# Delta rule with one inversion: ordering the loads of the inverted blocks and the first products on them

## The chip, the cores and the metric

The kernel runs on one core of a Trainium2 chip. The metric is the device time of one execution in microseconds (us); the median of three runs of the kernel before is 1357.24 us. TensorE is called PE here, VectorE DVE, ScalarE ACT, GpSimd POOL and SyncE SP.

## What is computed

The program runs two blocks on 256 tokens of width 1024 (the first block on 272, with 16 meta tokens): a feed-forward layer, an mLSTM mixer and a feed-forward layer, and then a gated delta rule mixer, a convolution-gated feed-forward layer, sliding-window attention and another such feed-forward layer. Only the delta rule is touched. Its core in the reference, for each chunk of 64 tokens and each of 16 heads:

```python
m = jnp.where(strict, jnp.einsum('bnhcd,bnhsd->bnhcs', k_beta, k) * decay, 0.0)
t_mat = lax.linalg.triangular_solve(m + eye, eye, left_side=True, lower=True, unit_diagonal=True)
u = jnp.einsum('bnhcs,bnhse->bnhce', t_mat, v_beta)
w = jnp.einsum('bnhcs,bnhsd->bnhcd', t_mat, k_beta * jnp.exp(gc)[..., None])
```

A step over the chunks then uses `u` and `w`; a gated norm and an output projection follow.

## The kernel before, in words

**Weights.** All weights lie in one tensor, in halves of eight 128x128 tiles (512 KB). `load_half` (L159) starts the transfer of a half into one of four `raw` buffers (L164) and keeps the transfer in `lastw[0]`. ACT then casts the half to `whi` in two pieces (L172), and DVE or POOL subtracts to get `wlo` (L174), into one of five pairs of buffers. `wtile` (L195) asks for the half that is `LOOK` = 3 ahead of the one in use. In the delta-rule stage the transfers are issued by ACT (L1150 sets `wq[0]` to it), elsewhere by SP. `mm3` (L248) makes three products for each tile (L251 to L253) and keeps the last one in `lastmm[0]`.

**The delta-rule stage.** Four blocks of projections are made first; 44 more (each eight tiles, so one half, and 24 products) are fillers: the rest of k and q, then z, then v, 16 blocks of each of the last two. I call the v blocks V0 to V15. The output projection `op_all` (L1130) is the last filler: 16 halves, O0 to O15, each of which needs the result of one head. Three halves of the feed-forward layer behind it, N0 to N2, are asked for before the stage ends.

Beside them run chains. `front` (L960) makes the masked products and stores them to DRAM (`ud`). `invert` (L979) loads the 32x32 diagonal blocks (`B`) and inverts all 128 of them at once on POOL, in 31 steps of two operations (L986, L988); the inverses go to DRAM (`xyd`, two POOL transfers, L992), and two more buffers are cleared (L997). `levels(q8)` (L1006), for each of eight head pairs, starts two loads of its off-diagonal rows (L1009) and four loads of inverted blocks (L1012), both on SP's queue, and then doubles the blocks from 32 to 128 by products with X and Y (L1026, L1034, L1048, L1053), of which L1026 is the first. `solve` and `outp` follow (L1067 to L1124). There are three XY buffers, `XYB` and two halves of `XZ`, so levels 0 to 2 begin together when the inversion is marked done, and each later level waits for the level three before it.

A v block ends on ACT (L737), three DVE operations (L739), ACT (L757), DVE (L758), two transposes on PE (L808) and two ACT copies into `Vn` (L810).

**What sets the order.** `Weave` (L48) is a planner in Python: each filler step and each chain step has a cost, a latency and a due time, and the planner puts out a chain's step when its due time has come and filler steps in between. The inversion counts 54 + 9 us there (L39, L999). Until it is marked done, DVE splits all weights; with the same mark POOL takes the odd halves (`share`, L1002). The program so put out is then scheduled at compile time: within the limits of the data and of ordering edges, the scheduler may move an instruction ahead of others on its engine's queue. `after(first, then)` (L144) draws such an ordering edge (class NoSync), which by itself gives no wait on the chip.

Of the kernel before, what the change touches and what calls it, by code (L numbers as in the profile page):

```python
# [120 lines left out]
def stack_kernel(ctx, tc, w, xt, cols, rows, gw, baw, rel, kc, kb, out):  # L121
    nc = tc.nc
    V, S, P_, T_ = nc.vector, nc.scalar, nc.gpsimd, nc.tensor
# [11 lines left out]
    def ps_mm(tag=None):  # L135
        if tag is None:
            rot[0] += 1
            tag = "st" if rot[0] % 3 == 0 else "mm"
        return pp.tile([128, 512], F32, name=tag, tag=tag, bufs=2 if tag == "st" else 4)
# [4 lines left out]
    def after(first, then):  # L144
        tc.add_manual_dep(then.ins, first.ins.name,
                          mybir.DependencyInfo(mybir.DependencyClass.NoSync, mybir.DependencyReason.DATA),
                          reason="order")

    lastw, lastmm = [None], [None]
# [567 lines left out]
    with tc.tile_pool(name="gd", bufs=1) as gp, tc.tile_pool(name="gw", bufs=2) as gq:  # L717
        def unit():
            return gp.tile([128, SEQ], F32, name="u1k", tag="u1k", bufs=67)
# [184 lines left out]
        def urows(g):  # L904
            return bass.AP(tensor=ud.tensor, offset=ud.offset + g * UG, ap=[[128, 128], [UG, 2], [1, 128]])
# [100 lines left out]
        def levels(q8):  # L1006
            u = [unit(), unit()]
            for j in range(2):
                nc.sync.dma_start(out=u[j], in_=urows(4 * q8 + 2 * j))  # L1009
            XY = xyt[q8 % 3]  # L1010
            for a in range(4):
                nc.sync.dma_start(out=XY[32 * a:32 * a + 32, :, 64 * a:64 * a + 64], in_=bass.AP(  # L1012
                    tensor=xyd.tensor, offset=xyd.offset + (16 * q8 + a) * 2048,
                    ap=[[64, 32], [4 * 2048, 4], [1, 64]]))
            fill.sp = max(fill.sp, fill.now) + 2.8
            xyv = XY.rearrange("p g (c t) -> p g c t", t=2)
            X, Y = xyv[:, :, :, 0], xyv[:, :, :, 1]
            yield 0.0, fill.sp + 2.0 - fill.now, 0.0
            def us(g, r0, nr, c0, ncl):
                return u[g // 2][r0:r0 + nr, (g % 2) * 128 + c0:(g % 2) * 128 + c0 + ncl]  # L1020

            r32 = unit()[:, 0:128].rearrange("p (g n) -> p g n", g=4)
            pr = ps_mm("mm")
            for b in (0, 64):
                for g in range(4):
                    T_.matmul(pr[b + 32:b + 64, g * 32:g * 32 + 32], us(g, b, 32, b + 32, 32), X[b:b + 32, g, b:b + 32],  # L1026
                              start=True, stop=True)
            for b in (32, 96):
                S.copy(r32[b:b + 32], pr[b:b + 32, 0:128].rearrange("p (g n) -> p g n", g=4))
            yield 0.5, 0.9, 0.0  # L1030
            px = ps_mm("mm")
            for b in (0, 64):
                for g in range(4):
                    T_.matmul(px[b:b + 32, g * 32:g * 32 + 32], r32[b + 32:b + 64, g, :],  # L1034
                              Y[b + 32:b + 64, g, b + 32:b + 64], start=True, stop=True)
                for g in range(4 if b == 0 else 0):
                    T_.matmul(px[b + 32:b + 64, g * 32:g * 32 + 32], Y[b + 32:b + 64, g, b + 32:b + 64],
                              r32[b + 32:b + 64, g, :], start=True, stop=True)
            for b in (0, 64):
                V.tensor_copy(Y[b:b + 32, :, b + 32:b + 64], px[b:b + 32, 0:128].rearrange("p (g n) -> p g n", g=4))  # L1040
                if b == 0:
                    V.tensor_copy(X[32:64, :, 0:32], px[32:64, 0:128].rearrange("p (g n) -> p g n", g=4))
            yield 1.0, 0.4, 0.9

            r64 = unit().rearrange("p (g n) -> p g n", g=4)
            pr = ps_mm("mm")
            for g in range(4):
                T_.matmul(pr[64:128, g * 64:g * 64 + 64], us(g, 0, 64, 64, 64), X[0:64, g, 0:64], start=True, stop=True)  # L1048
            S.copy(r64[64:128], pr[64:128, 0:256].rearrange("p (g n) -> p g n", g=4))
            yield 0.43, 0.7, 0.0  # L1050
            px = ps_mm("mm")
            for g in range(4):
                T_.matmul(px[0:64, g * 64:g * 64 + 64], r64[64:128, g, :], Y[64:128, g, 64:128], start=True, stop=True)  # L1053
            V.tensor_copy(Y[0:64, :, 64:128], px[0:64, 0:256].rearrange("p (g n) -> p g n", g=4))
            yield 0.43, 0.4, 0.42
            yield from solve(q8, Y)

        def solve(q8, Y):
            n21 = N21.pop(q8)
            pcs = [unit(), unit()]  # L1060
            pc = [pcs[g // 2][:, (g % 2) * 128:(g % 2) * 128 + 128] for g in range(4)]
            fill.need(("v", 2 * q8))
            fill.need(("v", 2 * q8 + 1))
            pw = ps_mm("mm")
            for j in range(2):
                vh = 2 * q8 + j
                T_.matmul(pw[:, j * 128:j * 128 + 128], Y[:, 2 * j], Vn[:, 0, vh, :], start=True, stop=True)  # L1067
                S.activation(out=pc[2 * j], in_=pw[:, j * 128:j * 128 + 128], func=AF.Copy,
                             scale=cc[:, 0, vh:vh + 1])
            yield 0.43, 1.0, 0.0  # L1070
            pw2 = ps_mm("mm")
            for j in range(2):
                T_.matmul(pw2[:, j * 128:j * 128 + 128], n21[:, j * 128:j * 128 + 128], pc[2 * j],
                          start=True, stop=True)
            V.tensor_tensor(out=Vn[:, 1, 2 * q8:2 * q8 + 2, :], in0=Vn[:, 1, 2 * q8:2 * q8 + 2, :],
                            in1=pw2[:, 0:256].rearrange("p (a b) -> p a b", a=2), op=ALU.subtract)
            yield 0.43, 0.4, 0.42
            pw3 = ps_mm("mm")
            for j in range(2):
                vh = 2 * q8 + j  # L1080
                T_.matmul(pw3[:, j * 128:j * 128 + 128], Y[:, 2 * j + 1], Vn[:, 1, vh, :], start=True, stop=True)
                S.activation(out=pc[2 * j + 1], in_=pw3[:, j * 128:j * 128 + 128], func=AF.Copy,
                             scale=cc[:, 1, vh:vh + 1])
            fill.mark("y", q8)
            yield 0.43, 1.0, 0.0
            yield from outp(q8, pc)
# [69 lines left out]
        for q8 in range(8):  # L1156
            cond = [("i",)]
            if q8 >= 3:
                cond.append(("y", q8 - 3))
            fill.chains.append((cond, levels(q8)))  # L1160
# [277 lines left out]
```

## Time and profile before

| | |
|---|---|
| median of 3 runs | 1357.24 us (1354.59 to 1360.41) |
| profiled execution | 1363.15 us, span 1361.4 us |
| PE, PE weight load | 95%, 93% of the span busy |
| DVE, ACT, POOL | 67%, 57%, 9% |
| mean granted TensorE clock | 0.971 of full |
| delta-rule stage | about 560 to 880 us of the span |

The span is what the profiler saw between the first and the last instruction. Busy shares are averages over the whole span; what the change touches lies in one stage, so the stage's own stretches, waits and queues are what is to be read.

### The profile page before, as it was taken

What the parts mean: (1) busy time and instruction counts of PE and PEld (TensorE: products, weight loads), DVE (VectorE), ACT (ScalarE), POOL (GpSimd) and SP (SyncE); (2) the same over time, 40 slices, a digit from 0 to 9 for tenths busy, and PEclk for the clock granted to TensorE, in tenths of its full rate; (3) what the DMA queues carried; (4) which work ended last, traced back from release to release, by engine and by line L of the source; (5) the groups of instructions that cost most, each with busy time, mean ns of one, the idle gap of its engine ahead of it and who ended that gap; (6) DMA issues with size and microseconds to landing.
All of it is one profiled execution on the core that took longest, in us unless ns stands there. A gap on an engine that the chain in (4) does not pass through costs nothing.

```text
span 1361.4 us, 27159 instructions
## 1 busy us (share of the span) xinstructions
PE 1298.9 (95%) x10665; PEld 1259.9 (93%) x10665; DVE 914.1 (67%) x1727; ACT 780.0 (57%) x1805; POOL 129.0 (9%) x149
## 2 busy tenths in 40 slices
PE   9999999999999999999973899999999999999997
PEld 8999999988999999899973789999999988999997
DVE  7866547775777753686662744698896575998852
ACT  7555446654765543556642645676675576777640
POOL 0000000000000000034493102201100000000000
PEclk9999999999999999999996879999999999999998
DMA  7755543532465554224733442468877431466650
GB/s 256 243 173 176 178 155 128 157 122 78 161 212 187 187 186 138 66 94 133 209 101 108 130 124 82 127 172 221 223 215 234 158 107 63 156 222 199 187 167 32
DMA packets 76064, 213.36 MB, mean 157 GB/s; under 512 B 16613, under 2 KB 25349, under 8 KB 75808
## 3 DMA queue, kind: packets, MB, share of 16 engines
q1 hardware_dynamic: 65248, 175.78, 40.9%
q10 hardware_dynamic: 8928, 31.99, 7.4%
q0 software_dynamic: 1760, 3.86, 1.6%
q8 instruction: 84, 1.38, 0.4%
q14 instruction: 44, 0.36, 0.1%
HBM read 207.00 MB, written 4.59 MB: 155 GB/s over the span
## 4 chain that ended last, share of the span: by engine, by line
PE 84%; DMA 4%; POOL 4%; DVE 3%; ACT 3%; issue 2%; SPq 0%; ACTq 0%; DVEq 0%; POOLq 0%
PE mm L251 13%; PE mm L253 12%; PE mm L252 12%; PE st L251 7%; PE st L252 7%; PE st L253 7%; DMA raw<-in_w 3%; PE mm L269 2%; PE mm L271 2%; PE mm L273 2%; POOL Z L988 2%; POOL tmp L986 2%; PE st L269 1%; PE st L273 1%; PE st L271 1%
## 5 line engine op out<-in xcount | busy, mean ns | idle before, releaser
L172 ACT CAST whi<-raw 128x512 fp32r<-128x512 f32 x752 | 435.8, 616 | 319.6 <-PE mm L252 107.0
L174 DVE TENSOR_TENSOR wlo<-raw,whi 128x1024 fp32r<-128x1024 f32 (+1 forms) x358 | 438.0, 1225 | 156.2 <-ACT whi L172 145.2
L251 PE MATMUL mm<-xh,whi 128*128 128x256 f32 (+1 forms) x1072 | 305.4, 285 | 1.3 <-ACT xh L380 1.3
L253 PE MATMUL mm<-xh,wlo 128*128 128x256 f32 (+1 forms) x1072 | 304.6, 284 | 0.0
L252 PE MATMUL mm<-xl,whi 128*128 128x256 f32 (+1 forms) x1072 | 304.2, 284 | 0.1
L251 PEld LDWEIGHTS mm<-xh,whi 128*128 128x128 f32 x1072 | 202.8, 189 | 3.1 <-ACT xh L380 2.2
L251 PE MATMUL st<-xh,whi 128*128 128x256 f32 (+1 forms) x704 | 202.1, 287 | 1.5 <-DVE gy L739 1.3
L252 PEld LDWEIGHTS mm<-xl,whi 128*128 128x128 f32 x1072 | 202.5, 189 | 0.5 <-DVE xl L381 0.5
L253 PEld LDWEIGHTS mm<-xh,wlo 128*128 128x128 f32 x1072 | 202.7, 189 | 0.1
L253 PE MATMUL st<-xh,wlo 128*128 128x256 f32 (+1 forms) x704 | 201.3, 286 | 0.0
L252 PE MATMUL st<-xl,whi 128*128 128x256 f32 (+1 forms) x704 | 201.0, 286 | 0.0
L251 PEld LDWEIGHTS st<-xh,whi 128*128 128x128 f32 x704 | 134.6, 191 | 2.6 <-DVE gy L739 1.5
L253 PEld LDWEIGHTS st<-xh,wlo 128*128 128x128 f32 x704 | 134.4, 191 | 0.1
L252 PEld LDWEIGHTS st<-xl,whi 128*128 128x128 f32 x704 | 134.5, 191 | 0.0
L251 PE MATMUL mm<-hh,whi 128*128 128x256 f32 (+1 forms) x352 | 99.5, 283 | 0.0
L252 PE MATMUL mm<-hl,whi 128*128 128x256 f32 (+1 forms) x352 | 99.4, 282 | 0.0
L253 PE MATMUL mm<-hh,wlo 128*128 128x256 f32 (+1 forms) x352 | 99.4, 282 | 0.0
L174 POOL TENSOR_TENSOR wlo<-raw,whi 128x1024 fp32r<-128x1024 f32 x19 | 45.3, 2384 | 500.4 <-ACT whi L172 434.2
L251 PEld LDWEIGHTS mm<-hh,whi 128*128 128x128 f32 x352 | 67.0, 190 | 0.0
L252 PEld LDWEIGHTS mm<-hl,whi 128*128 128x128 f32 x352 | 66.5, 189 | 0.0
L253 PEld LDWEIGHTS mm<-hh,wlo 128*128 128x128 f32 x352 | 66.5, 189 | 0.0
L440 DVE SCALAR_TENSOR_TENSOR fu<-mm,colt,fu 128x255 f32<-128x255 f32 x108 | 51.3, 478 | 14.5 <-ACT fu L437 14.4
(504 smaller groups left out, 2672.8 us busy)
## 6 DMA issues: line engine op xcount, KB each, us to landing
raw<-in_w SPq DMA_DIRECT2D x317, 512.0 KB, 4.4
raw<-in_w ACTq DMA_DIRECT2D x60, 512.0 KB, 3.8
ud<-u1k SPq DMA_DIRECT2D x16, 128.0 KB, 3.4
u1k<-ud SPq DMA_DIRECT2D x16, 128.0 KB, 3.2
Tb<-bvd POOLq DMA_DIRECT2D x16, 128.0 KB, 5.9
gx<-in_w SPq DMA_DIRECT2D x2, 512.0 KB, 6.7
xyd<-Z POOLq DMA_DIRECT2D x2, 512.0 KB, 5.3
h<-in_xt SPq DMA_DIRECT2D x3, 272.0 KB, 6.1
```

The lines of the kernel that those rows point to most:

```text
L172: S.copy(hi[:, c[0]:c[1]], raw[:, c[0]:c[1]])
L174: (P_ if share[0] and u % 2 else V).tensor_tensor(out=lo[:, c[0]:c[1]], in0=raw[:, c[0]:c[1]], in1=hi[:, c[0]:c[1]].bitcast(F32), op=ALU.s ...
L251: T_.matmul(ps, hi, xhh, start=first, stop=False)
L252: T_.matmul(ps, hi, xll, start=False, stop=False)
L253: lastmm[0] = T_.matmul(ps, lo, xhh, start=False, stop=last)
L269: T_.matmul(pss[j], wts[j][0], xhh, start=(k == 0), stop=False)
L271: T_.matmul(pss[j], wts[j][1], xhh, start=False, stop=False)
L273: T_.matmul(pss[j], wts[j][0], xll, start=False, stop=(k == kt - 1))
L440: V.scalar_tensor_tensor(out=t[:, d:], in0=ps[:, :T - d], scalar=wc(2 - d), in1=t[:, d:], op0=ALU.mult, op1=ALU.add)
L986: P_.tensor_tensor(out=t, in0=X[:, i, 0:i + 1].unsqueeze(1).to_broadcast([128, n, i + 1]), in1=B[:, i, i + 1:32].unsqueeze(2).to_broadcast ...
L988: P_.tensor_tensor(out=X[:, i + 1:32, 0:i + 1], in0=X[:, i + 1:32, 0:i + 1], in1=t, op=ALU.add)
```

## The change

Two ordering edges are added in `levels`. Each of the four loads of inverted blocks of a level is ordered behind the weight load put out last at that point, and the first of the eight L1026 products of each level (b = 0, g = 0) is ordered behind the last product of `mm3` put out by then. No instruction, size or buffer changes.

```diff
             for a in range(4):
-                nc.sync.dma_start(out=XY[32 * a:32 * a + 32, :, 64 * a:64 * a + 64], in_=bass.AP(
+                ins = nc.sync.dma_start(out=XY[32 * a:32 * a + 32, :, 64 * a:64 * a + 64], in_=bass.AP(
                     tensor=xyd.tensor, offset=xyd.offset + (16 * q8 + a) * 2048,
                     ap=[[64, 32], [4 * 2048, 4], [1, 64]]))
+                after(lastw[0], ins)
...
             for b in (0, 64):
                 for g in range(4):
-                    T_.matmul(pr[b + 32:b + 64, g * 32:g * 32 + 32], us(g, b, 32, b + 32, 32), X[b:b + 32, g, b:b + 32],
-                              start=True, stop=True)
+                    ins = T_.matmul(pr[b + 32:b + 64, g * 32:g * 32 + 32], us(g, b, 32, b + 32, 32), X[b:b + 32, g, b:b + 32],
+                                    start=True, stop=True)
+                    if b == 0 and g == 0:
+                        after(lastmm[0], ins)
```

## Rows read from the trace of the kernel before

**Rows 1.** Page, 40 slices of 34 us: busy tenths of PE in each.
```profile
PE   9999999999999999999973899999999999999997
```
**Rows 2.** PE's waits, whole span: line, what it waited for, us, times, longest.
```profile
PE ax L808 <- DVE gy L758: 32.8, 2, 29.6
```
**Rows 3.** Waits of DVE and of ACT, 660 to 900 us.
```profile
DVE gy L758 <- ACT vs L757: 31.6, 4, 30.1
ACT Vn L810 <- DMA XZ<-xyd: 31.9, 1, 31.9
ACT u1k L391 <- DVE gyo L1121: 15.8, 12, 3.3
```
**Rows 4.** Timeline of ACT and its queue at the stall: start, us, what [idle before].
```profile
702.09 0.47 ACT L737 ACTIVATE gy<-st,colt 128x256 f32<-128x256 f32 x1
734.08 0.34 ACTq L164 DMA_DIRECT2D raw<-in_w  x1
734.46 0.37 ACT L810 ACTIVATE Vn<-ax,nkh 128x128 f32<-128x128 f32 x1 [31.90 <-DMA XZ<-xyd]
734.63 0.38 ACTq L164 DMA_DIRECT2D raw<-in_w  x1
```
**Rows 5.** Timeline of SP's queue and of POOL at the end of the inversion.
```profile
728.24 2.91 SPq L1012 DMA_DIRECT2D XYB<-xyd  x4
731.00 1.83 POOL L997 MEMSET XZ<- 128x1024 f32 x2 [5.88 <-DMA xyd<-Z]
731.97 3.63 SPq L1012 DMA_DIRECT2D XZ<-xyd  x8
```
**Rows 6.** The chain that ended last, 724 to 735 us: start, us, what.
```profile
732.32 1.74 DMA XZ<-xyd
```
**Rows 7.** Stretches: length, then busy us of PE, PEld, DVE, ACT, POOL, clock, DMA.
```profile
682.60:702.50 19.90, 19.90 (x170) 19.74 (x169) 18.89 (x28) 13.40 (x32) 18.41 (x20) 1.00 0.46 148
705.90:735.90 30.00, 0.36 (x4) 0.15 (x2) 0.48 (x2) 1.29 (x4) 18.71 (x33) 0.54 0.22 49
735.90:764.90 29.00, 27.28 (x222) 26.33 (x223) 22.71 (x39) 18.40 (x46) 0.00 (x0) 0.95 0.53 168
764.90:798.00 33.10, 26.22 (x297) 23.21 (x296) 16.61 (x42) 21.44 (x75) 4.70 (x2) 0.73 0.48 143
798.00:876.60 78.60, 78.09 (x739) 73.85 (x737) 39.28 (x74) 39.56 (x127) 16.70 (x7) 0.94 0.31 97
```
**Rows 8.** PE's groups, 735 to 766 us: products of the v blocks, one of three.
```profile
L251 PE MATMUL st<-xh,whi 128*128 128x256 f32 x48 | 14.5, 301 | 1.3 <-DVE gy L739 1.3
L251 PE MATMUL ax<-xh,whi 128*128 128x256 f32 x16 | 4.5, 280 | 0.0
```
**Rows 9.** Line 737, 684 to 703 us: durations min/median/max in ns, first and last start.
```profile
L737 ACT ACTIVATE gy<-st,colt x4: 471/473/475, 685.2 to 702.1; 128x256 f32<-128x256 f32 x4
L737 ACT ACTIVATE gy<-ax,colt x2: 457/465/473, 688.3 to 697.0; 128x256 f32<-128x256 f32 x2
```
**Rows 10.** Lines 164 and 174, 733 to 878 us: weight loads on ACT, splits on POOL.
```profile
L164 ACTq DMA_DIRECT2D raw<-in_w x26: 334/334/381, 734.1 to 866.7; - x26
L174 POOL TENSOR_TENSOR wlo<-raw,whi x9: 2337/2382/2406, 767.1 to 871.7; 128x1024 fp32r<-128x1024 f32 x9
```
**Rows 11.** Timeline of ACT, 750 to 765 us: weight loads and v blocks' ends.
```profile
754.93 0.82 ACTq L164 DMA_DIRECT2D raw<-in_w  x2
...
760.77 0.33 ACTq L164 DMA_DIRECT2D raw<-in_w  x1
...
762.45 0.47 ACT L737 ACTIVATE gy<-ax,colt 128x256 f32<-128x256 f32 x1
```
**Rows 12.** Timeline of PE: first products of level 0, and the products behind them.
```profile
740.76 0.59 PE L1026 MATMUL mm<-XYB,u1k 32*32 32x32 f32 x16
...
765.23 0.34 PE L1034 MATMUL mm<-XYB,u1k 32*32 32x32 f32 x5
```
**Rows 13.** Page, DMA issues: KB each, median us from issue to landing.
```profile
raw<-in_w ACTq DMA_DIRECT2D x60, 512.0 KB, 3.8
```

## The prediction

> **What bounds the kernel now.** I read the slices first: PE is full nearly everywhere, and the one hole of the whole program is in slices 21 to 23 [rows 1]; its granted clock is 0.54 there [rows 7]. So the kernel is bound by PE's work, and time can be had only where PE stands. PE's waits name the hole: the transposes of a v block (L808) waited 29.6 us for DVE, in one piece, of 32.8 us of such waits in the program [rows 2]. That releaser is only the last link. DVE in turn waited 30.1 us for ACT's tanh, and ACT waited 31.9 us ahead of a copy into Vn, which needs nothing from DRAM, for a load of inverted blocks, XZ<-xyd [rows 3]. ACT's own timeline shows why: the instruction that stands ahead of that copy is a weight load, issued at 734.08 [rows 4]. The first XZ load leaves SP at 731.97 and lands at 732.32 + 1.74 = 734.06 [rows 5, 6]. The next weight load leaves at 734.63, half a microsecond later [rows 4]. I read that so: ACT's weight load carries a wait on a load of SP's, which stands some places earlier in the scheduled order of transfers. Twelve loads of blocks (levels 0 to 2) left SP's queue together, four XYB and eight XZ [rows 5]; the first XZ is the fifth of twelve, and the weight load would be the thirteenth, eight places on. The second weight load fits the sixth. The blocks themselves cannot come sooner: POOL writes the inverses out, clears XZ from 731.00 on, and only then do the XZ loads go [rows 5]. So ACT, DVE and PE stood for the end of the inversion, though the eight v blocks that were left need nothing of it. In the hole PE worked 0.36 of 30 us and DMA was busy 0.22 of the time [rows 7].
>
> The rule that speaks against this reading is the Trainium skill's, Trainium Kernel Development and Optimization, section Key Constraints: transfers issued by SP, ACT and POOL run on the same 16 DMA engines and interleave. By it, two queues meet in bandwidth, and moving an order between them would give no time at all; with DMA at 0.22 in the hole the trace does not agree that bandwidth was what ACT lacked. What it would give, 1357 us, is the second rival below.
>
> **The change part by part.** It removes and adds no instruction; 32 edges on loads and 8 on first products move things.
>
> *The edges on loads, levels 0 to 2.* Which load is "put out last" there? The same mark that lets the levels start gives POOL the odd halves. After the hole 26 weight loads are left on ACT and POOL makes nine splits, the first at 767.1 [rows 10]. 26 are V9 to V15, O0 to O15 and N0 to N2; of the last 19 nine have odd numbers in the tensor (O1 is the first, V15 is odd too and was split by DVE). So the mark falls after V15's load was put out, which is when V12 starts, and before O1's, when V14 starts; counting the planner's costs through gives the middle of V13, so the edge is to O0's load. All loads that the v blocks need then stand ahead of the twelve loads of blocks, and the wait moves from V9's load to O1's, or further.
>
> What that gives: PE has eight v blocks left after the hole (64 products of one kind in 735 to 766 [rows 8]). Ahead of the hole six blocks ended on ACT in 702.1 - 685.2 = 16.9 us, five steps of 3.4 us [rows 9], with DVE at 18.89 of 19.90 us and PE full [rows 7]. At that pace the last eight take PE from 705.9 to 705.9 + 8 x 3.4 = 733, against 764.9 now. The last block's product end moves by up to 32 us.
>
> What is late next: first O1's load. In the trace it left ACT at 760.77, just ahead of V13's end on ACT at 762.45 [rows 11]. V13 would end on ACT at 702.1 + 8 x 3.4 = 729, so ACT comes to O1's load near 727 and stands until the XZ load lands at 734.1: some 7 us for ACT, and 5 for PE (in the trace 31.9 on ACT made 29.6 on PE). From there on everything runs as it did from 760.77: a shift of 760.77 - 734.08 = **26.7 us**. If O0's load is what waits (the second of the pair at 754.93, so about 755.3 [rows 11]), the shift is 21. If the wait falls behind O1's, the blocks' landing bounds it: the XZ loads leave SP until 735.6 [rows 5] and land 1.7 us later, 737.3, where now the second products of level 0 (L1034) start at 765.23 [rows 12], so 28, and with level 0 going ahead alone (its four loads leave by 731.2 [rows 5]) up to 31. I take 27, the nearest to the rows, and 21 to 31 as its ends.
>
> *The edges on loads, levels 3 to 7.* They are put out when O2's or O3's load was, by the same count; these loads need no buffer that the levels hold, and are long gone when the XY buffers of levels 0 to 2 come free. Cost 0; covered by that buffer wait. If the cover is gone, a load of blocks waits for one weight load, 3.8 us each [rows 13].
>
> *The edges on first products.* Level 0's went ahead of V9's last product at 740.76, yet its result was used at 765.23 [rows 12], after all v blocks. Behind V14's products it still is in time: 0, with 24 us of cover. Levels 1 and 2 are behind V14 and V15 already. For levels 3 to 7 the last product put out is V15's or one of O0's or O1's. The trace has no such wait; bounds: 0, and one block of the output projection, 24 products at 19.9 us / 170 = 0.12 us [rows 7], 3 us for each of five, which only counts where PE stands for it. PE works 78.09 of 78.6 us from 798 on [rows 7], so I take 0, and keep -5 for the range.
>
> *The clock.* The mean of 0.95 in 735.9 to 764.9 [rows 7] means some 2.9 us at half clock (1.2 GHz), so 1.4 us of work lost after the hole. A shorter stand may still halve it: between 0 and +1.4, I take 0. The levels' stretch, at 0.73, and the next, at 0.94 [rows 7], I leave as they are; either could move by 3 us in either direction.
>
> *SP and POOL.* SP's queue keeps its order: loads of rows, twelve loads of blocks, loads of rows for level 3. POOL does the same work. The sum is -27.
>
> **Base.** The profiled execution took 1363.15 us with a span of 1361.4 us; the median of the runs shown is 1357.24, 0.4% lower. I take the shift, which is one wait long, over to the median: 1357.2 - 27 = **1330**. The profiled execution would come to 1336.
>
> **The rivals.**
>
> *A longer stand stays* (gain 8 to 20, about 1343). The scheduler could put O0's or O1's load earlier on ACT than now. It can't before V13's half is split, since there are four raw buffers, and that is at 720 by the same pace; then ACT stands 14 us and PE 12, and the gain is 18; with DVE's backlog behind it less. For it: ACT issues V9's load well ahead of its use. Against: rows 11 have these loads late.
>
> *The edges do not decide* (1357). An edge from ACT's queue to SP's is no wait, and if the scheduled order of the transfers does not change, nothing does. For it: the other uses of `after` in the kernel pair instructions of one engine. Against: the wait in rows 3 and 4 is itself made of such an order.
>
> *More is given back* (gain 33 to 38, about 1322). PE stood 6.9 of 33.1 us in the levels' stretch [rows 7]; if the last v blocks fall into it, some of that is filled.
>
> *Slower* (about 1368). One mechanism: the first products of levels 3 to 7 stand on PE's queue behind products of the output projection, and those wait for the heads' last splits; then each level pays its predecessor's end in series. Such an end showed 3.3 us at the longest (ACT's L391 waiting for DVE's L1121 [rows 3]). It decides against the gain only where five levels lose over 27/5 = 5.4 us each, and by 0.5% at 6.8 us; 8 us each would give 1330 + 40 = 1370. Against: PE is full from 798 on [rows 7], with such products between those of the levels.
>
> **How the numbers follow.** Forecast 0.62; longer stand 0.17; more given back 0.08; edges do not decide 0.08; slower 0.05. The forecast's own range is 1326 to 1337 (31 and 21 less, with clock). The range of 1321 to 1347 takes in the longer stand and most of "more", and leaves out the last two cases and an edge, some 0.16. About 0.5%, 6.8 us, is what a measurement of this kernel can tell from no change; faster than 1350.5 has 0.88, within 0.07, slower than 1364 0.05.
>
> **What would show it.** In the changed kernel: V9's load on ACT's queue before 705 and no wait of over 15 us of ACT for XZ or XYB; PE's wait at L808 down from 29.6 to under 12 us; all v products done by 743; the twelve block loads still at 728 to 736, since POOL's part is the same; the first L1034 at 735 to 744; the stage's end, and all behind it, earlier by the shift. I am wrong if ACT's wait is as long in front of another load, if SP's block loads leave later than 736, or if PE's stands return in front of L1026 or in the output projection.

## The result, and the profile after

The change takes the median from 1357.40 to 1341.87 us (four runs of each): a ratio of 0.9888, with an interval of 0.9856 to 0.9921. It is faster by more than 0.5%, and by 15.5 us where 27 were forecast. The program was measured twice more, once under another edit that compiles to the same order (1341.61 against 1360.20) and once as it is (1342.52 against 1364.40), so its gain lies between 15.5 and 21.9 us, and the forecast was too large by 5 to 12. The profiled execution took 1343.67 us, span 1341.9, mean granted clock 0.979 (before: 1363.15, 1361.4, 0.971). The times of the stage below come from one profile of each program; where the change has three profiles, the text gives all three.

The page's slices after, PE, answering to [rows 1]. The hole of three slices is now a dent of three.

```profile
PE   9999999999999999999998889999999999999997
```

Waits of PE and of ACT after, 660 to 900 us (line, what it waited for, us in total, times, longest), answering to [rows 2, 3]:

```profile
PE mm L1027 <- DMA XYB<-xyd: 4.9, 3, 3.5
PE st L251 <- DVE gy L739: 3.2, 2, 3.0
PE ax L808 <- ACT Vn L810: 2.9, 1, 2.9
PE ax L808 <- DVE gy L758: 0.9, 2, 0.5
...
ACT vs L757 <- DVE gy L739: 16.4, 11, 3.4
ACT Vn L810 <- PE ax L808: 10.1, 4, 8.0
```

The 31.9 us of ACT for XZ and the 29.6 us of PE at L808 are gone. (The change adds lines, so L1026 is L1027 after, and L1034 is L1037.) But a wait that was not there stands first: PE in front of the first product on the inverted blocks.

The timeline after of ACT's weight loads and of two v blocks' ends on ACT (V5 and V13, as in [rows 9, 11]), of POOL and of SP's queue (start, us, what, idle before), answering to [rows 4, 5, 11]:

```profile
702.59 0.33 ACTq L164 DMA_DIRECT2D raw<-in_w  x1
...
704.13 0.47 ACT L737 ACTIVATE gy<-st,colt 128x256 f32<-128x256 f32 x1
...
733.50 0.34 ACTq L164 DMA_DIRECT2D raw<-in_w  x1
...
735.21 0.47 ACT L737 ACTIVATE gy<-ax,colt 128x256 f32<-128x256 f32 x1
...
743.77 0.34 ACTq L164 DMA_DIRECT2D raw<-in_w  x1
...
736.81 1.83 POOL L997 MEMSET XZ<- 128x1024 f32 x2 [6.08 <-DMA xyd<-Z]
...
733.90 3.13 SPq L1012 DMA_DIRECT2D XYB<-xyd  x4
737.78 4.14 SPq L1012 DMA_DIRECT2D XZ<-xyd  x8
```

V9's load leaves at 702.59, where it stood until 734.08 [rows 4]. O1's load leaves at 733.50, 27.3 us earlier than at 760.77 [rows 11]: the forecast's 26.7. But the block loads leave SP 5.7 us *later* than 728.24 and 731.97 [rows 5], and they are longer on the way. The chain that ended last, after (start, us, what), has the first of them:

```profile
733.90 5.04 DMA XYB<-xyd
```

It lands at 738.94. O1's weight load, issued at 733.50, was on the way then, and lands at 738.77. Before, no weight load was on the way, and the same block load took 2.8 us, from 728.24 to 731.05. So the first block is there 7.9 us later than before: 5.7 from leaving later and 2.2 from the longer way.

The timeline after of PE around the first products of level 0, answering to [rows 12], and then the first instruction of the norm that ends the stage, before (first line) and after:

```profile
731.88 0.38 PE L251 MATMUL st<-xh,whi 128*128 128x256 f32 x1 [3.03 <-DVE gy L739]
739.08 0.60 PE L1027 MATMUL mm<-XYB,u1k 32*32 32x32 f32 x8 [3.46 <-DMA XYB<-xyd]
740.97 0.63 PE L1027 MATMUL mm<-XYB,u1k 32*32 32x32 f32 x8
745.62 0.34 PE L1037 MATMUL mm<-XYB,u1k 32*32 32x32 f32 x5
```
```profile
884.77 0.61 PE L344 MATMUL ax<-ones,acc 128*128 128x1 f32 x4
865.38 0.60 PE L344 MATMUL ax<-ones,acc 128*128 128x1 f32 x4
```

So the shift shrinks as one goes down the chain: 27.3 us at O1's load, 765.23 - 745.62 = 19.6 at level 0's second products, 19.4 at the stage's end, 1361.4 - 1341.9 = 19.5 in the span. All that is missing was lost before 746 us. Nothing is lost or won behind that.

The stretches after, as in [rows 7]:

```profile
705.90:735.90 30.00, 25.89 (x199) 24.21 (x197) 27.08 (x41) 18.00 (x44) 22.50 (x31) 0.96 0.55 160
735.90:764.90 29.00, 21.15 (x226) 19.16 (x227) 12.81 (x29) 13.49 (x37) 6.53 (x4) 0.63 0.38 109
764.90:798.00 33.10, 29.24 (x291) 26.95 (x290) 14.76 (x34) 15.55 (x58) 2.40 (x1) 0.80 0.39 119
```

PE works 25.89 us of the old hole (it was 0.36), and the low mean clock that the hole had (0.54) is now in the stretch behind it (0.63), where the recursion of the levels begins.

**Why the blocks come later.** POOL's groups of the inversion, first before, then after (busy us, mean ns of one), 660 to 760 us:

```profile
L988 POOL TENSOR_TENSOR Z<-Z,tmp 128x31 f32<-128x31 f32 (+15 forms) x31 | 22.2, 717 | 2.4
L986 POOL TENSOR_TENSOR tmp<-Z,B 128x31 f32<-128x31 f32 (+15 forms) x31 | 20.9, 674 | 13.2 <-DMA B<-ud 10.8
```
```profile
L988 POOL TENSOR_TENSOR Z<-Z,tmp 128x31 f32<-128x31 f32 (+15 forms) x31 | 26.8, 865 | 2.4
L986 POOL TENSOR_TENSOR tmp<-Z,B 128x31 f32<-128x31 f32 (+15 forms) x31 | 21.0, 679 | 13.6 <-DMA B<-ud 11.2
```

The same 62 operations ran from 673.04 to 720.94 before and from 673.81 to 726.46 after: 52.7 us in place of 47.9. Operation by operation the reason can be read. The same two operations of POOL, before (first two lines) and after, and what DVE did after:

```profile
709.73 0.68 POOL L988 TENSOR_TENSOR Z<-Z,tmp 128x231 f32<-128x231 f32 x1
711.12 0.66 POOL L988 TENSOR_TENSOR Z<-Z,tmp 128x220 f32<-128x220 f32 x1
```
```profile
710.48 1.56 POOL L988 TENSOR_TENSOR Z<-Z,tmp 128x231 f32<-128x231 f32 x1
712.83 1.53 POOL L988 TENSOR_TENSOR Z<-Z,tmp 128x220 f32<-128x220 f32 x1
...
709.85 1.63 DVE L174 TENSOR_TENSOR wlo<-raw,whi 128x1024 fp32r<-128x1024 f32 x1
712.44 1.39 DVE L174 TENSOR_TENSOR wlo<-raw,whi 128x1024 fp32r<-128x1024 f32 x1
```

Each POOL operation of over 1.1 us lies beside a split of DVE: 15 of 62 after, 10 of 62 before. Before, DVE stood idle from 705 on with everything else, so the last part of the inversion ran free. The stall had been speeding up the very work that it waited for.

### The profile page after: what moved, and what is told of

Its sections match the earlier page's. It is cut to its first block, busy times and chain, and to the rows that moved or that the text cites. A ratio compares the mean times of both kernels' runs of the same rounds, so it can differ in the third digit from the quotient of the medians.

```text
span 1341.9 us, 27160 instructions
## 1 busy us (share of the span) xinstructions
PE 1301.2 (97%) x10665; PEld 1260.8 (94%) x10665; DVE 919.1 (68%) x1727; ACT 780.2 (58%) x1805; POOL 134.0 (10%) x149
## 4 chain that ended last, share of the span: by engine, by line
PE 79%; DMA 6%; DVE 5%; ACT 4%; POOL 4%; issue 2%; SPq 0%; ACTq 0%; DVEq 0%; POOLq 0%
PE mm L251 11%; PE mm L253 11%; PE mm L252 11%; PE st L251 7%; PE st L252 7%; PE st L253 7%; DMA raw<-in_w 4%; PE mm L269 2%; PE mm L271 2%; PE mm L273 2%; POOL Z L988 2%; POOL tmp L986 2%; DVE wlo L174 2%; ACT whi L172 1%; PE st L269 1%
```

## The experiments

The theory that I took to the chip: (a) the time before was lost because ACT's weight load waited for a load of blocks of SP's, and the edges on loads alone remove that; (b) of the forecast's gain, part went because DVE's splits now lie beside the inversion, and part because PE meets the first product of level 0 before the blocks are there, with products of V14 and V15 queued behind it. The rivals: the edges on products do part of the work, the transfers only compete for bandwidth, POOL is slowed by something other than DVE, the stand of PE costs nothing.

**The edges on loads alone, and the edges on products alone.**

```diff
-                    if b == 0 and g == 0:
-                        after(lastmm[0], ins)
```

> Only the edges on the loads of inverted blocks; the first products carry no edge. Theory (the load edges do all of it): same as the full change, 1338 to 1346 us, ratio 0.986 to 0.991, first products of level 0 in the middle of V14, PE standing some 3.5 us in front of them. Rival (the product edges bring a part): at least 4 us slower than the full change, with first products of level 0 ahead of V14.

Measured: 1341.61, ratio 0.9861 (0.9836 to 0.9886). In the compiled order this program is the same as the change's, instruction for instruction, so its run is a second one of the change.

```diff
-                after(lastw[0], ins)
```

> Only the edges on the first products; the loads stay where they were in the order. Theory: ACT still waits over 28 us in front of a weight load for a load of blocks, PE still stands 29 us at L808, ratio 0.997 to 1.003. Rival (the order of products on PE is what counted): like the full change, ratio 0.986 to 0.991.

Measured: 1361.17, ratio 1.0001 (0.9983 to 1.0018). ACT's wait is there as before, if a little under the 28 us expected (PE's at L808 is 25.2):

```profile
ACT Vn L810 <- DMA XZ<-xyd: 26.6, 1, 26.6
```

The whole gain is that of the load edges. The product edges, for which the range held 5 us, change nothing once the load edges are there.

**What the wait is.** The compiled program shows it. Transfers of SP and of ACT take turns on eight completion counters (DMAHW0 to DMAHW7), and one that takes a counter waits until the counter's last transfer is done, unless its engine has already waited for that one. In the kernel before, the first of the eight XZ loads takes counter 2 and the second counter 3. Eight counters on, with one weight load among them, comes V9's:

```
before, SP:  L1012 DMA XZ<-xyd 32x4x64 [waits DMAHW2_49,DMASW4_49,Pool_49]
             L1012 DMA XZ<-xyd 32x4x64 [waits DMAHW3_49]
before, ACT: L737 ACTIVATE gy<-st,colt 128x256
             L164 DMA raw<-in_w 128x1024 [waits DMAHW3_49]
             L810 ACTIVATE Vn<-ax,nkh 128x128 [waits PE_49]
```

The traces bear it out to 0.02 us. Before, the second XZ load lands at 734.06 and V9's load leaves at 734.08; with the edges on products alone it is 734.77 and 734.79, and in the kernel before with a later mark (below) 729.92 and 729.94.

If that is the wait, the same block loads on a queue whose transfers use other counters need no edge at all:

```diff
-                ins = nc.sync.dma_start(out=XY[32 * a:32 * a + 32, :, 64 * a:64 * a + 64], in_=bass.AP(
+                nc.gpsimd.dma_start(out=XY[32 * a:32 * a + 32, :, 64 * a:64 * a + 64], in_=bass.AP(
...
-                after(lastw[0], ins)
```

> The loads of inverted blocks are issued by POOL and not by SP, without edges on loads; the product edges stay. Theory (SP's and ACT's transfers share a set of completion counters, POOL's have their own): no wait of ACT over 10 us for a load of blocks; twelve issues on POOL at 0.57 us put the last block 5 us later than in the changed kernel, so 0 to 8 us slower than that, 1342 to 1350 us, ratio 0.989 to 0.995. Rival (ACT's wait was for bandwidth or for data of the inversion): ACT waits 28 us or more again, ratio 0.997 to 1.003.

Measured: 1338.04, ratio 0.984 (0.9809 to 0.9871). ACT shows no wait on a block, though the loads have no edge. I had expected the time to be equal or worse; it is some 3 us better than the loads-only run of the same series, but the intervals overlap. Its PE stands 4.7 us in front of the first product:

```profile
736.98 1.68 POOL L1012 DMA_DIRECT2D XYB<-xyd  x3 [5.06 <-DMA xyd<-Z]
738.65 1.86 POOL L997 MEMSET XZ<- 128x1024 f32 x2
740.43 0.55 POOL L1012 DMA_DIRECT2D XYB<-xyd  x1
740.86 0.94 PE L1026 MATMUL mm<-XYB,u1k 32*32 32x32 f32 x16 [4.71 <-POOL XZ L997]
```

The profile puts the stand down to the clearing of XZ, but in the compiled program these products wait for the first and the third block load, and both left ahead of the clearing. The first left at 736.98, 3.1 us later than in the change, and landed at 740.77, just ahead of the products. The fourth, behind the clearing, landed only at 742.50, when they had run.

And if the wait is a matter of places in the order, a shorter move must give part of it back:

```diff
+    oldw = []
...
+            oldw[:] = oldw[-4:] + [lastw[0]]
...
-                after(lastw[0], ins)
+                after(oldw[-3] if q8 < 3 else lastw[0], ins)
```

> The block loads of levels 0 to 2 are ordered behind the weight load three halves earlier than in the change; all else as in the change. Theory (a weight load on ScalarE's queue that comes behind a block load in the order stands until that block has landed): ScalarE stands 8 to 18 us in front of a weight load near 722, PE idles 5 to 15 us before the blocks land near 737, and the time lies between the change and the kernel before: 1346 to 1354, ratio 0.990 to 0.996. Rival (what counts is only that the loads are not ahead of the whole row of weight loads): 1339 to 1344, no wait of ScalarE on a block over 2 us.

Measured: 1351.49, ratio 0.9913 (0.988 to 0.9945), the theory's number. ACT stands again, in front of a later weight load and shorter (its timeline, and PE's wait; the lines are shifted by two). In the compiled program that load takes the counter of the fourth XYB load, which lands at 741.73:

```profile
741.75 0.33 ACTq L166 DMA_DIRECT2D raw<-in_w  x1
742.13 0.62 ACT L812 ACTIVATE Vn<-ax,nkh 128x128 f32<-128x128 f32 x2 [11.96 <-DMA XYB<-xyd]
...
PE ax L810 <- ACT Vn L812: 12.6, 2, 11.9
```

**What slows the inversion.** While the inversion is put out, the low parts of the weights are not made, and the high part stands in for them; this leaves out those subtractions.

```diff
-        lo = pool.tile([128, 1024], F32R, name="wlo", tag="wlo")
+        lo = hi if nosplit[0] else pool.tile([128, 1024], F32R, name="wlo", tag="wlo")
...
-        for c in ((0, 512), (512, 1024)) if u == 0 else ((0, 1024),):
+        for c in () if nosplit[0] else ((0, 512), (512, 1024)) if u == 0 else ((0, 1024),):
```

> Leaves out the low parts (wlo) of the weight halves that are loaded between the start and the end of the inversion; the products take the high part in their place, so PE's work is the same and VectorE has one subtraction a half less. Theory: each 128x1024 subtraction of VectorE makes one GpSimd operation of the inversion some 0.95 us longer (15 of 62 over 1.1 us after the change, 10 before), so without them at most 3 of 62 are over 1.1 us, the 62 take 38 to 41 us in place of 52.6 and the first block load leaves SP between 719 and 725 in place of 733.9. PE then has no stand in front of level 0's first product that is over 1 us. Time 1331 to 1342. Rival (GpSimd is slowed by transfers or by ScalarE's copies, not by VectorE): 12 or more of 62 stay over 1.1 us, the inversion takes 50 to 54 us, the first load leaves at 731 to 736, time 1338 to 1346.

Measured, in one execution: 1337.19. POOL's groups (L988 and L986 are L990 and L988 here), the end of its work, SP's first block loads, and level 0's first product on PE:

```profile
L990 POOL TENSOR_TENSOR Z<-Z,tmp 128x31 f32<-128x31 f32 (+15 forms) x31 | 18.2, 587 | 2.4
L988 POOL TENSOR_TENSOR tmp<-Z,B 128x31 f32<-128x31 f32 (+15 forms) x31 | 15.7, 507 | 12.6 <-DMA B<-ud 10.3
...
712.04 0.25 POOL L990 TENSOR_TENSOR Z<-Z,tmp 128x31 f32<-128x31 f32 x1
...
720.33 2.97 SPq L1015 DMA_DIRECT2D XYB<-xyd  x4
...
734.12 0.43 PE L1030 MATMUL mm<-XYB,u1k 32*32 32x32 f32 x8
```

None of the 62 operations is over 1.1 us, they take 712.29 - 673.61 = 38.7 us in place of 52.7, and the blocks leave 13.6 us earlier. 52.7 - 38.7 = 14 us for 15 operations is 0.93 us each, and 47.9 - 38.7 = 9.2 for 10 is 0.92: the price of a split holds in both kernels. PE does not stand in front of level 0's first product, as expected (its longest wait for a block, 1.5 us, is at a later level, at 767). The total is 6.5 us less than in the profiled run of the change, but since work is left out here that number also holds DVE's relief, and it is one execution.

**What the stand in front of the first product costs.** The planner puts level 0 out when it takes the inversion for done. In the change the first product then stands behind 21 of V14's 24 products on PE's queue, with the last three and V15's 24 behind it. A later mark puts it behind V15's products, with the same edges:

```diff
-INVERT_COST = 54.0
+INVERT_COST = 60.0
```

> The full change, and the planner counts the inversion 6 us longer (60 for 54), so that the levels are put out later and the first products of level 0 stand behind V15 and not in V14. Theory (part of the missing gain is PE standing in front of those products with V14 and V15 behind it): no stand of over 1 us in front of them before V15 is done, 3 to 5 us faster than the full change, ratio 0.984 to 0.987; the first load of blocks leaves at 732 to 736 us as in the changed kernel. Rival (only the landing of the blocks counts): same as the full change within 1.5 us.

Measured: 1337.36, ratio 0.9824 (0.979 to 0.9857), 4.3 us under the loads-only run of the same series, with overlapping intervals. To settle whether that is a gain, a series on one chip with the change itself, this mark again, one between (57), and the mark without the edges:

> The change itself, beside the two marks on the same chip: 1340 to 1344, ratio 0.985 to 0.990. Its profiled run shows PE standing 2 to 7 us in front of level 0's first product again, and 13 to 16 of GpSimd's 62 operations over 1.1 us.

> The mark at 60 a second time. If the stand in front of level 0's first product is what the change still loses, 1335 to 1340, at least 2 us under the change in this same series. If the first look was luck, 1340 to 1344, no difference from the change.

> The change with the mark at 57. In the compiled order level 0's first product already stands behind V14's products here, as at 60. Theory (the stand is the loss): as at 60, 1335 to 1340, PE waits at most 3 us in front of the first product. Rival (the gain at 60 comes from the later levels and not from the stand): between 54 and 60 or like 54, 1340 to 1344.

> The kernel before with the mark at 60 and none of the change's edges. Theory: the blocks' loads keep their place ahead of the last weight loads, ScalarE still waits 25 to 35 us for a block, and the later mark alone gives nothing: 1354 to 1362, ratio 0.996 to 1.002. Rival (a later mark is worth 4 us by itself, whatever the loads do): 1351 to 1355.

Measured: the change 1342.52 (0.9835, 0.9804 to 0.9866), mark 60 1335.41 (0.9783, 0.9754 to 0.9811), mark 57 1339.62 (0.9802, 0.9771 to 0.9832), the kernel before with mark 60 1363.00 (0.9992, 0.9965 to 1.002). The profiled run of the change stands 4.6 us at L1027 again. With mark 60 PE's timeline (V15's last product first) and the stage's end are:

```profile
740.35 0.28 PE L253 MATMUL st<-xh,wlo 128*128 128x256 f32 x1
...
741.03 0.43 PE L1027 MATMUL mm<-XYB,u1k 32*32 32x32 f32 x8
741.75 0.43 PE L1027 MATMUL mm<-XYB,u1k 32*32 32x32 f32 x8 [0.29 <-DMA XYB<-xyd]
...
745.43 0.47 PE L1037 MATMUL mm<-XYB,u1k 32*32 32x32 f32 x5 [1.90 <-ACT u1k L1032]
...
860.45 0.61 PE L344 MATMUL ax<-ones,acc 128*128 128x1 f32 x4
```

Level 0's second products start at the same time as in the change, but PE has done V15's products by 740.6, where in the change the last of them starts at 745.2; the stage ends at 860.45, 24.3 us earlier than before and 4.9 earlier than in the change's first profile. The stage's start moves by a few us from profile to profile. Counted from the inversion's first operation, its end comes after 211.7 us before, after 191.6, 190.1 and 192.7 in the three profiles of the change, after 186.7 and 186.0 in the two of mark 60, and after 185.0 with mark 57. So the mark at 60 beats both kernels: the change by 4.3 us in the first series and by 7.1 in the second, where the intervals overlap slightly, but each of its six executions is below each of the change's six. The mark without the edges gives nothing (its 1363.00 is 1 us above the expected times, its ratio inside the expected one), and ACT waits 27.6 us for XZ.

The mark at 57 lies between in time, and its interval overlaps both others. Its PE stands 2.8 us in front of the first product, yet V14's and V15's products are all ahead of the stand there, and the stage is as short as at 60. That points to the 27 products behind the stand, more than to the stand itself.

How much of the 4 to 7 us that is stays open. By 746 us PE has worked as long in the change as with mark 60 (25.89 and 6.92 us in the stretches to 735.9 and to 746, against 26.15 and 6.98), because with mark 60 it stands elsewhere, 1.90 us of it in front of the second products; but its mean granted clock from 735.9 to 746 is 0.62 in the change and 0.84 with mark 60, and from 764.9 to 798 it is 0.80 and 0.90. The mark also decides which odd halves POOL splits (one in place of two there by 760 us). No run separates these.

Later still, and both remedies together:

> The change with the planner's mark for the inversion at 66 in place of 54. Theory: with 60 PE's stand in front of level 0's first product is already gone, so a still later mark gives nothing more and starts the recursion's chain later: 1335 to 1342. Rival (the stand was not what 60 took away, and the later the products the better): 1326 to 1334.

Measured: 1343.24, ratio 0.9877 (0.9857 to 0.9896): 1 us above what was expected and no better than the change. PE stands 3.1 us in front of the first product, and level 0's second products start at 746.63. Of the four marks tried 60 gave the lowest time, 57 could not be told from it, and at 60 the first product meets the blocks as they land.

> The block loads on GpSimd's queue, without load edges, and the planner's mark for the inversion at 60 in place of 54. Theory: the two gains overlap (both only keep the first product off PE's queue until the blocks are there), so 1332 to 1339, ratio 0.979 to 0.984, and PE has no wait over 2 us in front of level 0's first products. Rival (GpSimd's own issues, some 0.55 us each, put the blocks later than SP does): 1339 to 1344.

Measured: 1339.43, ratio 0.9841 (0.9813 to 0.9869), no better than the POOL queue alone. PE stands 6.3 us in front of the first product, so my expectation missed: the first block load leaves POOL at 737.35 and lands at 741.09, and the products start at 741.18; the later mark does not bring the blocks sooner.

## Why the prediction was right and where it failed

**The bound and the wait: right.** The hole was ACT's queue behind a weight load that waits for a block load of SP's; what I read from [rows 2 to 6] stands but for the count. Bandwidth as the cause of ACT's stand, and the rival that the edges do not decide, fall with the loads-only run, the POOL queue and the shorter move. The count was off by one: the transfer waited for is the sixth of the twelve loads, and it is V9's load, the first one, that waits for it. I had given it the fifth, and read the landing at 734.06 [rows 6] as the fifth's: in the trace the fifth lands at 733.58 and the sixth at 734.06. I had also taken the second weight load's 734.63 [rows 4] for the sixth's follower. That load carries no wait on a counter; it only stood behind the first one on ACT's queue.

**The new place of the loads, and the shift at O1's load: right in size, not in mechanism.** 27.3 us for the 26.7 forecast. But I had ACT stand 7 us at O1's load. In the compiled program O1's load carries no wait on a counter, and O2's waits for counter 3, that of the first XZ load, which left at 737.78; O2's load left at 743.77, and no wait of ACT on a block shows. ACT never stood for a block. What held O1's load back was the pace of the v blocks: from V5's end on ACT at 704.13 to V13's at 735.21 a block took 3.9 us, where I had carried 3.4 over from a stretch ahead of the hole [rows 9]. V13 ended 6.2 us later than the 729 that I had worked out, and that took the place of the 7 us that I had given the stand. So the agreement of 27.3 with 26.7 is luck: two errors cancel. Why the pace is 3.9 stays open; without the splits it is the same (31.0 us for these eight blocks, 31.1 in the change), so DVE's splits alone do not set it. The rival "longer stand" gave about 1343, near the measured 1341.87, but its mechanism, ACT standing at O0's or O1's load, is not what happened either.

**The step that failed first: "POOL does the same work", "the twelve block loads still at 728 to 736".** They left between 733.90 and 741.9, so one of the prediction's own signs of being wrong, block loads that leave later than 736, came up. I took the inversion's length from a trace in which DVE stood idle for its last 16 us. Five more splits beside it at 0.93 us make 4.7 us; measured 52.7 - 47.9 = 4.8. The rule stood in the Trainium skill, SBUF — State Buffer, section SBUF: two separate sides: an operation of VectorE with two SBUF inputs and one of GpSimd that reads SBUF take one port pair in turn, and the loser blocks for the whole instruction. Both are such operations here, and the trace agrees in kind: POOL's operation went from 0.68 to 1.56 us, and the split beside it took 1.39 to 1.63 us, where splits ahead of the inversion take 1.22. The way of the blocks was mis-sized beside it. The bound of 737.3 carried the 1.7 us of one load [rows 6] over to the last of the twelve; that one landed at 740.02 even before, and at 743.36 after. The first block's way grew from 2.8 to 5.0 us beside O1's load, and it landed 7.9 us later.

**The step that failed second: "0, with 24 us of cover" for the first products.** The cover was the age of a result at the place where the old kernel used it. Once the v blocks move up by 27 us, the cover moves with them: 24 us of cover against 27 us of shift leaves none, and with the first block 7.9 us late PE stood 3.5 us (4.6 and 6.8 in the other two profiles of the same program), with the rest of V14 and V15 on its queue behind the stand, in a stretch with a mean clock of 0.63, a mix of the two levels (1.2 and 2.4 GHz). The 26.7 us at O1's load became 19.6 at L1037. PE's stand in front of the first product was the other sign of being wrong that the prediction named. The later mark gives the size of this term, with what else the mark moves: 4.3 and 7.1 us in the medians of two series.

**What was left at 0 and held:** levels 3 to 7, whose product edges do nothing in the compiled order; the output projection; the stretch from 765 on. The v products were to be done by 743 and L1037 to start by 744; PE still made V products at 745.2, and L1037 came at 745.62. No run shows the "slower" rival.

**The sum.** Span to span: 26.7 forecast, 19.5 measured, and 24.3 at the stage's end in a profile of mark 60, where no product of the v blocks waits behind the first product. What is left of 26.7, some 2 us, is no more than profiles of one program differ by; it may be the blocks' lateness: without the splits the span is 1335.4, 26.0 under that of before, but that run leaves work out, so this part is argued and not shown. That the time fell into the range is in part luck: its upper part was kept for a stand of ACT, and what filled it was one of PE.

## What to carry to other kernels

A wait that sits on an issuing engine can come from transfers of another queue that only share its completion counters; look at which transfer, a fixed number of places back, lands just then, and move the late transfers behind those that others need. When a stall is taken away, everything that was measured inside it has to be priced anew: work that ran alone there gets company, and cover that was counted from the old end of the stall is used up by the shift itself. After such a change, set the planner's due times again: here that was worth a quarter to a third of the change's own gain (4.3 of 18.6 us, 7.1 of 21.9).

## What I had not expected of the hardware

A subtraction of 128x1024 by DVE (1.22 us ahead of the inversion) costs a POOL operation beside it 0.92 to 0.93 us in the mean, whatever that operation's own size: the smallest of the fifteen took 1.18 us (0.31 in the kernel before), the largest some 1.6 (0.73). The subtraction itself grows to between 1.4 and 1.8 us beside most of them. The 62 operations of the inversion take 38.7 us without such subtractions, 47.9 beside ten such subtractions and 52.7 beside fifteen.

The first block load lands just behind a weight load that is on the way when it leaves. In the nine profiles with such a weight load it landed 0.16 to 0.46 us behind it, after 3.7 to 6.9 us; in the five without one it took 2.0 to 2.8 us. The two come from different queues, ACT's and SP's or POOL's. No run moves the weight load alone, so that it is what delays the block is read from the times and not shown by an experiment.
